# The table builder's powers go from the shared constants tile to the scratch tile of the attention

## The chip, the cores and the metric

The kernel runs on one core of a Trainium2 chip. TensorE (PE) multiplies matrices, VectorE (DVE) and ScalarE (ACT) work elementwise, GpSimd (POOL) does elementwise work too, and SyncE (SP) only starts transfers; POOL and ACT have transfer queues of their own. Each engine works through its instructions in order, and waits for another engine by a semaphore, a counter that the other engine raises. The metric is the device time of one launch in microseconds (us), as a median over runs: 3279.76 us for the kernel before, from three runs between 3275.04 and 3284.11. A difference under about 0.3% (10 us) can't be told from none.

## The reference

One sequence of 1024 tokens with 1024 channels goes through two transformer layers and then a third block, all in float32. Layer 0 mixes with forgetting attention and multi-scale pooling, layer 1 with a gated linear recurrence, and each is followed by a gated feed-forward network (FFN). The third block has an mLSTM branch and an S5 branch, a complex linear recurrence whose coefficients are computed from the inputs:

```
x = x + rmsnorm(mixer(rmsnorm(x, mix_pre_g)), mix_post_g)               # layers 0 and 1
x = x + rmsnorm((silu(h @ w_gate) * (h @ w_up)) @ w_down, ffn_post_g)   # h = rmsnorm(x, ffn_pre_g)
dt   = exp(log_dt);  mag = exp(lam_re * dt)                             # S5: parameters alone, no x
a_re = mag * cos(lam_im * dt);  a_im = mag * sin(lam_im * dt)
s_t  = a * s_(t-1) + B u_t;  y_t = Re(C s_t) + D u_t                    # complex, per group and state
```

The coefficients of S5 depend on the parameters alone, so their tables can be built at any time before the third block.

## The kernel before, in words

The channels lie on the 128 partitions and the tokens on the free axis. The 1024 tokens are two halves of 512, and a 128 x 512 tile of float32 is the unit of nearly all work. A matrix product is made of three passes: each operand is split into a rounded part and its remainder (ACT writes the first, DVE the second), and TensorE multiplies high by high, high by low and low by high. In the down projection of the FFN these are lines 632, 633 and 634; weights come in as `raw`, are split into `wsp` at lines 186 and 188, and the hidden activations `hid` are split at lines 246 and 250.

The program is written in Python generators. A main line emits the matmuls, and background generators (`start`, `tick`, `drain`) emit a few instructions of other work between them. A scheduler then sets the order on each engine and hands out memory. Tiles of one tag share a fixed number of slots: the 18 slots of `t2` (128 x 512 float32 each) hold the transfers of the hidden activations (`xt`, read by `fetch` at line 260), the temporaries `sq` and the two tiles `s5c`. A new tile in a slot must wait until every instruction that touched the tile before it there is done, whichever engine that was.

FFN 0 ends with its down projection (`ffn_down`), for token half 0 and then for half 1. The products for half 1 need 22 `hid` tiles, and each comes from a transfer `xt<-hidd` that SP issues (`hid_steps`). Beside the projection of half 0 runs the table builder, `s5_tables`:

- It takes two `s5c` tiles from `t2` (line 1239) as a pool of 64 small vectors of 16 columns; `sm(name)` hands them out in turn. POOL clears both tiles (line 1241).
- DVE computes small vectors in them, among them the eight powers `E` (real and imaginary parts, 16 vectors), each the square of the one before (lines 1281 to 1297).
- POOL builds the rotation tables `s5R` from `E` by doubling, in eight passes of two groups each. A pass clears the first column (lines 1319 and 1320), multiplies in eight steps of six instructions (lines 1326 to 1331; 1326, 1327, 1329 and 1330 read `E`), and stores two tables to DRAM by its own queue (line 1335).
- At the end SP stores the two `s5c` tiles to DRAM (line 1338); `s5_tables2` loads them later.

The tag `junk` has one slot of 1024 bytes per partition. The attention of layer 0 writes its masked scores there at line 986, where only the maximum that goes with them is used; nothing else has it before the change.

Of the kernel before, what the change touches and what calls it, by code (L numbers as in the profile page):

```python
# [11 lines left out]
F32 = mybir.dt.float32  # L12
# [55 lines left out]
class Model:  # L68
# [1166 lines left out]
    def s5_tables(self):  # L1235
# [8 lines left out]
        def sm(n):  # L1244
            i = self.s5n[n] = len(self.s5n)
            return big[i // 32][:, i % 32]
# [31 lines left out]
        V.tensor_tensor(t0, mag, mag, ALU.mult)  # L1278
        V.tensor_tensor(self.rho4, t0, t0, ALU.mult)

        E = [(sm(f"er{k}"), sm(f"ei{k}")) for k in range(8)]
        cur = (cs, sn)
        for k in range(-2, 8):
            o = E[max(k, 0)]
            if k > -2:
# [32 lines left out]
        for g0 in range(0, 16, 2):  # L1318
            G.memset(R[:, :, 0, 0:1], 1.0)
            G.memset(R[:, :, 1, 0:1], 0.0)  # L1320
            for k in range(8):
                n = 1 << k
                er, ei = (E[k][i][:, g0:g0 + 2].unsqueeze(2).to_broadcast([128, 2, n]) for i in range(2))
                s, d = slice(0, n), slice(n, 2 * n)
# [713 lines left out]
```

## Time and profile before

| | us |
|---|---|
| median of 3 runs | 3279.76 |
| the profiled execution: its own time / its span | 3275.86 / 3274.2 |
| PE busy in the span | 3099.3 (95%) |
| DVE / ACT / POOL busy | 2345.7 / 1532.8 / 803.9 |
| mean granted TensorE clock, as a share of 2.4 GHz | 0.978 |

The profile cuts the span into 40 slices of 81.9 us and gives the busy tenths of each engine. The waits say who was idle, and whose end ended the idle time; the wait of a transfer queue is told apart from the engine's own. The time line lists single instructions with their start, and the idle time ahead of them in brackets. Nearly all of the idle time of PE lies in two neighbouring slices, between 982 and 1146 us, and they are the place where the down projection of FFN 0 goes from half 0 to half 1.

### The profile page before, as it was taken

How to read it: one execution, taken by the hardware profiler on the slowest of the kernel's cores; microseconds unless marked ns; L12 is line 12 of the kernel's file. 1: busy time of each engine (PE TensorE's matmuls, PEld its weight loads, DVE VectorE, ACT ScalarE, POOL GpSimd, SP SyncE). 2: the span in 40 equal slices, each digit the busy share in tenths (PEclk: the TensorE clock that was granted, in tenths of full speed). 3: DMA queues.
4: the chain of work that ended last, by engine and by line, in shares of the span. 5: the costliest groups of instructions: out<-in, count | busy, mean ns of one | idle time of the engine just before them, and what ended most of it. 6: DMA issues, size and time to landing. Idle time of an engine off the chain costs nothing. (4 is left out here: it accounts for less than half of the span.)

```text
span 3274.2 us, 42443 instructions
## 1 busy us (share of the span) xinstructions
PE 3099.3 (95%) x14200; PEld 2526.0 (77%) x14200; DVE 2345.7 (72%) x4489; ACT 1532.8 (47%) x2842; POOL 803.9 (25%) x1002
## 2 busy tenths in 40 slices
PE   8999999999994598999999999999999999999998
PEld 5777787888883487877888887777888778778886
DVE  8768857688862359777857888786688888765664
ACT  4646644333432237676443335544455444434442
POOL 4011102555367302111236540000111100153000
PEclk9999999999997799999999999999999999999999
DMA  4443445333532434334723345576644344745562
GB/s 156 157 143 127 145 153 191 103 126 126 191 115 103 151 121 150 101 125 162 253 93 130 126 144 191 199 226 240 214 136 154 129 153 136 257 140 196 187 209 97
DMA packets 227179, 511.84 MB, mean 156 GB/s; under 512 B 28040, under 2 KB 50760, under 8 KB 226960
## 3 DMA queue, kind: packets, MB, share of 16 engines
q1 hardware_dynamic: 225680, 504.93, 46.2%
q0 software_dynamic: 1280, 4.20, 0.3%
q8 instruction: 112, 1.84, 0.2%
q14 instruction: 107, 0.88, 0.1%
HBM read 386.21 MB, written 118.59 MB: 154 GB/s over the span
## 5 line engine op out<-in xcount | busy, mean ns | idle before, releaser
L188 DVE TENSOR_TENSOR wsp<-raw,wsp 128x512 fp32r<-128x512 f32 x850 | 629.8, 747 | 350.5 <-ACT wsp L186 347.2
L186 ACT ACTIVATE wsp<-raw 128x512 fp32r<-128x512 f32 x842 | 515.7, 616 | 722.5 <-PE pd L634 201.5
L632 PE MATMUL pd<-hid,wsp 128*128 128x512 f32 x704 | 279.2, 398 | 76.6 <-ACT hid L246 76.6
L633 PE MATMUL pd<-hid,wsp 128*128 128x512 f32 x704 | 278.9, 397 | 3.5 <-DVE hid L250 3.2
L634 PE MATMUL pd<-hid,wsp 128*128 128x512 f32 x704 | 277.6, 394 | 0.0
L632 PEld LDWEIGHTS pd<-hid,wsp 128*128 128x128 f32 x704 | 133.9, 190 | 105.6 <-ACT hid L246 78.7
L495 PE MATMUL qy<-st,wsp 128*128 128x512 f32 x464 | 180.7, 389 | 3.9 <-DVE st L248 3.9
L494 PE MATMUL qy<-st,wsp 128*128 128x512 f32 x464 | 181.1, 390 | 0.2 <-ACT st L246 0.2
L496 PE MATMUL qy<-st,wsp 128*128 128x512 f32 x464 | 180.6, 389 | 0.0
L526 POOL TENSOR_TENSOR qv<-qv,qu 128x512 f32<-128x512 f32 x54 | 90.6, 1677 | 341.8 <-ACT wsp L186 226.6
L633 PEld LDWEIGHTS pd<-hid,wsp 128*128 128x128 f32 x704 | 133.9, 190 | 37.3 <-DVE hid L250 10.1
L248 POOL TENSOR_TENSOR xs<-xt,xs 128x512 fp32r<-128x512 f32 x28 | 40.8, 1457 | 483.6 <-ACT xs L246 424.8
L634 PEld LDWEIGHTS pd<-hid,wsp 128*128 128x128 f32 x704 | 134.0, 190 | 26.9
L186 ACT ACTIVATE wsp<-wss 128x512 fp32r<-128x512 f32 x108 | 68.1, 631 | 183.9 <-PE qz L496 90.3
L494 PE MATMUL pf<-xs,wsp 128*128 128x512 f32 x288 | 114.0, 396 | 9.5 <-ACT m L572 8.5
L270 DVE TENSOR_TENSOR sq<-sq 128x512 f32<-128x512 f32 x140 | 99.0, 709 | 32.1 <-ACT sq L268 31.6
L250 DVE SCALAR_TENSOR_TENSOR hid<-xt,hid 128x512 fp32r<-128x512 f32 x88 | 58.0, 689 | 84.3 <-ACT hid L246 83.6
L495 PE MATMUL pf<-xs,wsp 128*128 128x512 f32 x288 | 113.3, 394 | 0.4 <-POOL xs L248 0.4
L496 PE MATMUL pf<-xs,wsp 128*128 128x512 f32 x288 | 113.3, 394 | 0.0
L405 POOL TENSOR_TENSOR xt<-xt,m 128x512 f32<-128x512 f32 x12 | 18.2, 1524 | 364.9 <-DVE m L402 356.7
L495 PEld LDWEIGHTS qy<-st,wsp 128*128 128x128 f32 x464 | 87.1, 188 | 22.1 <-DVE st L248 4.2
L494 PEld LDWEIGHTS qy<-st,wsp 128*128 128x128 f32 x464 | 87.1, 188 | 20.3 <-DVE qu L515 1.8
(720 smaller groups left out, 9106.3 us busy)
## 6 DMA issues: line engine op xcount, KB each, us to landing
raw<-in_w_in_dram SPq DMA_DIRECT2D x86, 512.0 KB
xt<-xres SPq DMA_DIRECT2D x128, 256.0 KB
raw<-in_wd_dram SPq DMA_DIRECT2D x64, 512.0 KB
raw<-in_wg_dram SPq DMA_DIRECT2D x62, 512.0 KB
raw<-in_wu_dram SPq DMA_DIRECT2D x62, 512.0 KB
hidd<-th SPq DMA_DIRECT2D x88, 256.0 KB
xt<-hidd SPq DMA_DIRECT2D x88, 256.0 KB
raw<-in_ev_in_dram SPq DMA_DIRECT2D x32, 512.0 KB
```

Of the source, the lines that this page charges most:

```text
L186: nc.scalar.activation(sp[:, 0], raw, AF.Copy)
L188: nc.vector.tensor_tensor(sp[:, 1], raw, f(sp[:, 0]), ALU.subtract)
L248: (low or nc.vector).tensor_tensor(t[:, 1], src, f(t[:, 0]), ALU.subtract)
L250: nc.vector.scalar_tensor_tensor(t[:, 1], src, scale, f(t[:, 0]), ALU.mult, ALU.subtract)
L270: nc.vector.tensor_tensor(q, q, acc, ALU.add)
L494: nc.tensor.matmul(ps, h, xs[k][:, 0], start=start and k == 0, stop=False, skip_group_check=not start)
L495: nc.tensor.matmul(ps, h, xs[k][:, 1], start=False, stop=False, skip_group_check=not start)
L496: nc.tensor.matmul(ps, l, xs[k][:, 0], start=False, stop=k == n - 1, skip_group_check=not start)
L526: nc.gpsimd.tensor_tensor(v5, v5, u3, ALU.add)
L632: nc.tensor.matmul(ps, h_, x[:, 0], start=k0 + k == 0, stop=False)
L633: nc.tensor.matmul(ps, h_, x[:, 1], start=False, stop=False)
L634: nc.tensor.matmul(ps, l_, x[:, 0], start=False, stop=k0 + k == FFT - 1)
```

## The change

The eight powers no longer come from the `s5c` tiles. They lie in one tile of their own, `s5e`, of 16 vectors of 16 float32, which is 1024 bytes per partition; it has the tag `junk` and so the slot of the attention's scratch.

```diff
         V.tensor_tensor(t0, mag, mag, ALU.mult)
         V.tensor_tensor(self.rho4, t0, t0, ALU.mult)
 
-        E = [(sm(f"er{k}"), sm(f"ei{k}")) for k in range(8)]
+
+        et = self._t([128, 16, 16], F32, "junk", 1, "s5e")
+        E = [(et[:, 2 * k], et[:, 2 * k + 1]) for k in range(8)]
         cur = (cs, sn)
         for k in range(-2, 8):
             o = E[max(k, 0)]
```

Lines behind it move down by two. With 16 names fewer, `sm` hands out 17 vectors in all, so that the second `s5c` tile holds none; it is still cleared and stored. The instructions are the same in number, kind and shape on all engines, and the order on PE, DVE, ACT and POOL is the same, but for names. What differs is on whom some of them wait, and the place of one transfer on SP.

The first place is SP's queue, at the transfers of half 1 of the hidden activations (`hidd_15` is the 16th of 22; names such as DMAHW4 stand for transfer semaphores):

```order
 L260 DMA xt<-hidd_13_201 128x512 [waits DMAHW2_49]
 L260 DMA xt<-hidd_14_202 128x512 [waits DMAHW3_49]
-L260 DMA xt<-hidd_15_203 128x512 [waits DMAHW4_49,Pool_49]
+L260 DMA xt<-hidd_15_203 128x512 [waits DMAHW4_49]
 L260 DMA xt<-hidd_16_204 128x512 [waits DMAHW5_49,DVE_49]
 L260 DMA xt<-hidd_17_205 128x512 [waits DMAHW6_49,PE_49]
```

Nothing moved; the 16th transfer no longer waits for POOL, because POOL no longer reads the tile whose slot it takes.

The second place is DVE, in the residual addition behind the down projection of half 0 (line 405):

```order
 L188 TENSOR_TENSOR wsp<-raw,wsp 128x256 [waits Activation_49]
 L405 TENSOR_TENSOR xt<-xt,m 128x512 [waits DMAHW0_49,DVE_49]
-L405 TENSOR_TENSOR xt<-xt,m 128x512 [waits DMAHW1_49,DVE_49]
+L405 TENSOR_TENSOR xt<-xt,m 128x512 [waits DMAHW1_49,DVE_49,Pool_49]
 L402 SCALAR_TENSOR_TENSOR m<-m,pvt,rb 128x512 x2
 L188 TENSOR_TENSOR wsp<-raw,wsp 128x512 [waits DMAHW3_49,Activation_49]
```

One addition now waits for POOL too; before, DVE had waited for the same count at line 1304, where it wrote into the second `s5c` tile after POOL's clearing.

The third place is SP's queue earlier, in the middle of the down projection of half 0, where the two `s5c` tiles are stored (`s5c_675` is the second one's place in DRAM):

```order
 L175 DMA raw<-in_wd_dram 128x768 [waits DMAHW5_49,DVE_49]
-L175 DMA raw<-in_wd_dram 128x1024 [waits DMAHW6_49,DMAHW3_49,DVE_49]
-L1338 DMA s5c_675<-s5c 128x512 [waits DMAHW7_49,DVE_49]
+L1340 DMA s5c_675<-s5c 128x512 [waits DMAHW6_49,Pool_49]
+L175 DMA raw<-in_wd_dram 128x1024 [waits DMAHW7_49,DMAHW3_49,DVE_49]
 L175 DMA raw<-in_wd_dram 128x1024 [waits DMAHW4_49,DMAHW0_49,DVE_49]
```

The store of the second tile has moved ahead of one load of weights.

## Rows read from the trace of the kernel before

**Rows 1.** The page's 40 slices of the span: PE's busy tenths and granted clock.
```profile
PE   8999999999994598999999999999999999999998
PEclk9999999999997799999999999999999999999999
```

**Rows 2.** Windows: start:end, length, busy of PE, PEld, DVE, ACT, POOL; clock, DMA.
```profile
1100.00:1150.00 50.00, 49.92 (x207) 40.26 (x208) 31.35 (x50) 21.35 (x39) 0.00 (x0) 0.94 0.68 229
1150.00:1200.00 50.00, 50.00 (x227) 41.28 (x227) 22.83 (x44) 17.99 (x31) 1.81 (x2) 1.00 0.42 138
```

**Rows 3.** Waits, 950 to 1200 us: who waited for whom, total us, times, longest.
```profile
ACT hid L246 <- DMA xt<-hidd: 75.5, 4, 73.1
...
PE pd L632 <- ACT hid L246: 72.2, 1, 72.2
```

**Rows 4.** Waits of SP's transfer queue, 950 to 1200 us.
```profile
SPq L260 <- POOL s5rt L1330: 86.3, 1, 86.3
```

**Rows 5.** Time line of POOL at the tables' end: start, us, instruction, idle before.
```profile
1096.13 0.61 POOL L1330 TENSOR_TENSOR s5rt<-s5R,s5c 128x256 f32<-128x256 f32 x1
...
1097.84 1.13 POOL L1335 DMA_DIRECT2D s5r<-s5R  x2 [0.30 <-POOL s5R L1331]
1171.44 1.29 POOL L248 TENSOR_TENSOR xs<-xt,xs 128x512 fp32r<-128x512 f32 x1 [72.47 <-ACT xs L246]
```

**Rows 6.** Time line of SP's transfer queue at the join of the halves.
```profile
1096.77 3.62 SPq L260 DMA_DIRECT2D xt<-hidd  x7
```

**Rows 7.** Time line of PE around its long wait.
```profile
1027.52 0.40 PE L634 MATMUL pd<-hid,wsp 128*128 128x512 f32 x1
1100.08 0.80 PE L632 MATMUL pd<-hid,wsp 128*128 128x512 f32 x1 [72.17 <-ACT hid L246]
...
1101.40 0.63 PE L634 MATMUL pd<-hid,wsp 128*128 128x512 f32 x1
1101.83 0.63 PE L632 MATMUL pd<-hid,wsp 128*128 128x512 f32 x1
...
1106.50 0.40 PE L632 MATMUL pd<-hid,wsp 128*128 128x512 f32 x1
1106.73 0.39 PE L633 MATMUL pd<-hid,wsp 128*128 128x512 f32 x1
```

**Rows 8.** Waits of PE, 1990 to 2241 us: the same projection of FFN 1.
```profile
PE pd L632 <- ACT hid L246: 4.2, 1, 4.2
...
PE pd L633 <- DVE hid L250: 0.4, 1, 0.4
```

**Rows 9.** Windows over the multiplications of five of POOL's eight passes.
```profile
940.88:960.65 19.77, 19.77 (x89) 16.38 (x88) 6.47 (x10) 6.43 (x12) 17.00 (x50) 1.00 0.34 107
965.97:985.91 19.94, 19.94 (x90) 16.51 (x89) 6.26 (x10) 5.63 (x10) 17.17 (x50) 1.00 0.33 99
991.23:1010.82 19.59, 15.77 (x68) 12.51 (x66) 7.33 (x14) 8.24 (x14) 16.82 (x50) 0.92 0.60 205
1016.35:1036.00 19.65, 11.56 (x45) 8.16 (x43) 7.64 (x12) 6.59 (x12) 17.25 (x49) 0.85 0.00 1
1061.02:1077.77 16.75, 0.00 (x0) 0.00 (x0) 0.00 (x0) 0.00 (x0) 13.97 (x50) 0.50 0.00 0
```

**Rows 10.** Time line of POOL, start of passes 5 and 7, and the last clearing of s5c.
```profile
884.11 0.53 POOL L1241 MEMSET s5c<- 128x512 f32 x1 [0.75 <-DVE th L603]
...
1016.35 0.10 POOL L1319 MEMSET s5R<- 128x2 f32 x1 [4.39 <-DMA s5r<-s5R]
...
1061.02 0.10 POOL L1319 MEMSET s5R<- 128x2 f32 x1 [2.17 <-DMA s5r<-s5R]
```

**Rows 11.** Time line of PE at the first product of layer 1.
```profile
1212.86 0.39 PE L236 MATMUL pxr<-xs,wsp 128*128 128x512 f32 x1
```

**Rows 12.** Line groups of DVE by shape, 966 to 1011 us, then 1140 to 1170 us.
```profile
L188 DVE TENSOR_TENSOR wsp<-raw,wsp 128x512 fp32r<-128x512 f32 x14 | 10.3, 737 | 24.6 <-ACT wsp L186 24.6
...
L188 DVE TENSOR_TENSOR wsp<-raw,wsp 128x512 fp32r<-128x512 f32 x10 | 6.9, 692 | 10.4 <-ACT wsp L186 10.4
```

## The prediction, made blind

> **What bounds the kernel now.** I read the page's slices first. PE is busy in nine tenths or more of nearly every slice and at its full granted clock, so that TensorE sets the time, but for two neighbouring slices that show 4 and 5 tenths and a clock of 0.7 [rows 1]. Any change away from them touches engines that run under PE. So the question is what ends last in that hole, and the waits answer it from engine to engine: PE at line 632 waits 72.2 us for ACT's split of a hidden tile, ACT has waited 73.1 us for the transfer that brings that tile [rows 3], and the queue that starts the transfer has itself stood 86.3 us, once, for POOL at line 1330 [rows 4]. The time line closes the chain: POOL's last multiplication by a power ends at 1096.13 + 0.61 = 1096.74 us [rows 5], and SP starts the seven missing transfers at 1096.77 [rows 6]. The transfer did not want anything that POOL makes. It wanted the memory of a tile that POOL was still reading. All of POOL's passes from the fifth on are paid by everyone else.
>
> **The change, part by part.**
>
> *The wait that goes.* POOL's multiplications no longer read the `s5c` tile, so that its slot comes free when DVE has written it and SP has stored it. SP came to the 16th transfer at 1096.77 - 86.3 = 1010.5 us, and nothing behind it in that queue could start. In the changed program it goes on there. PE's idle time of 72.2 us between 1027.9 and 1100.08 [rows 7] goes with it, if the seven tiles are there in time. They are 7 x 256 KB = 1.8 MB, and around 1000 us the transfers moved 205 GB/s [rows 9], which makes 9 us: landed by about 1020 to 1023, and a split of one tile takes about 0.7 us (line 188 in [rows 12] has the same shape). PE wants the first at 1027.9. Some of the seven still wait for DVE and PE, whose work is close behind. What such a join costs where POOL is not in the way is seen in FFN 1: 4.2 and 0.4 us [rows 8]; its larger part stands at the start of the half, which here lies before the long wait and does not change. Bounds for what is left of the join: 0 to 4.6 us. I take 0.5, nearer the smaller row, since 15 of 22 tiles are already there.
>
> *The clock.* During the hole the granted clock is 0.50, TensorE's level of 1.2 GHz [rows 9], and after it matmuls start 0.43 us apart (1101.40, 1101.83) until they start 0.23 apart (1106.50, 1106.73) [rows 7]. Of the 6.42 us from 1100.08 to 1106.50 the same 15 matmuls would have taken 15 x 0.23 = 3.4, so 3.0 us come back too.
>
> *Waits that are new.* The 4th addition at line 405 waits for POOL in the changed order. The count it asks for is the one that line 1304 asked for before, POOL's second clearing, and that was over at 884.11 + 0.53 us [rows 10], over 140 us before half 1 goes on. Price 0. The store of the second `s5c` tile goes one place forward in SP's queue and waits for that same clearing: 0 as well. The slot `junk` was last used in layer 0's attention, which is done before FFN 0 begins, so taking it costs no wait. Instructions, shapes and orders are otherwise the same.
>
> *What is late next.* The tables do not get shorter; they lose a quiet machine. Before, POOL's last passes ran while DVE was idle; now half 1 of the projection runs beside them. POOL's next duty behind the tables is the low part of the input of layer 1 (line 248), which PE needs at its first product of layer 1, at 1212.86 before [rows 11], so about 1212.86 - 74.7 = 1138.2 after. Is POOL done by then? With DVE idle the multiplications of a pass take 16.75 us. Four passes beside DVE took 19.77, 19.94, 19.59 and 19.65, with DVE busy 6.47, 6.26, 7.33 and 7.64 us [rows 9]. That is 0.47, 0.51, 0.39 and 0.38 us of delay for each us of DVE, 0.44 in the mean. What DVE did in the 100 us from 1100 (31.35 + 22.83 = 54.2 us; [rows 2]) it will do from 1028 on. POOL ended at 1097.84 + 1.13 = 1099.0 [rows 5]; 54.2 x 0.44 = 23.8 us are added, and three more waits for the store between passes that are 4.39 instead of 2.17 us [rows 10], 6.7 us together. End: 1129.5. The first low part (1.29 us, [rows 5]) is there at 1130.8, 7.4 us before PE asks. So this costs 0 at the rate of the rows. The rate at which it begins to cost is (1138.2 - 1.3 - 1099.0 - 6.7) us over DVE's 54.2 and some 4 us more that it has until 1138, about 0.54, just over the largest of the four. If every us of DVE held POOL for a whole one, POOL would end 1099.0 + 6.7 + 54.2 + some 4.6 (DVE's share up to 1138) = 1164.5, and PE would stand until 1165.8: 27.6 us. Those are the bounds, 0 and 27.6; I take 0, since four rows give the rate, and keep the other end for the range.
>
> The Trainium skill has a rule against this change just here. Its page "SBUF — State Buffer", section "Who interferes with whom", says that a VectorE instruction with two SBUF inputs and a GpSimd instruction that reads SBUF shut each other out for their whole length. DVE's splits and POOL's multiplications are such a pair. The trace agrees in direction, and less in size, with 0.44 us of delay for each us; by the rule at full strength the cost would be the upper bound, 27.6 us, and by the rows it is nothing.
>
> *The other direction.* DVE's splits at line 188 took 737 ns beside POOL and 692 without it [rows 12], 0.045 us more; for the 94 DVE instructions of the 100 us [rows 2] that would be 4 us at most. DVE stood idle 10.4 us beside ten such splits, waiting for ACT [rows 12], so this stays under cover; without that cover it would cost the 4 us.
>
> **The sum.** 72.2 + 3.0 - 0.5 = 74.7 us. The profiled execution took 3275.86 us, so it would take 3201.2. The median of the runs shown is 3.9 us higher, which gives 3205.1 by that; I take the middle, 3203.
>
> **The rivals.**
>
> *POOL is late* (the case above with a rate over 0.54). For it: the margin is 7.4 us, and DVE is denser in the new neighbourhood (31.35 of 50 us) than in any of the four passes from which the rate comes. Against: the cost begins softly, at a rate of 0.6 POOL is only some 4 us late. The page of the Trainium skill named above leads to its far end. Then PE waits at line 236 for POOL at line 248, up to 27.6 us: 3205 to 3229 against the execution's own time, 3233 against the median.
>
> *Another wait takes the place.* If the addition at line 405 asked for the end of the tables, DVE would stand in half 1 from a point before 1078 (the addition lies in the first 50 us behind the hole) until at least 1099 us, and with it the weight splits and PE: 21 to 71 us, so 3222 to 3272. For it: the wait is new. Against: the count belongs to the clearing at 884 us.
>
> *The change does not do what it says.* Were the 16th transfer held by POOL through some other tile, the time would stay at 3276 to 3280. For it: POOL also holds two tiles through all its passes (`s5R`, `s5rt`). Against: these lie in slots of their own, outside `t2`, and the wait is gone from the row of the order.
>
> *Slower than before.* DVE and POOL shut each other out in both directions through half 1. If each of the 94 DVE instructions in those 100 us were held by a whole long multiplication of POOL (0.61 us, [rows 5]) with no idle time to absorb it, PE would lose 94 x 0.61 = 57 us for weights, and with POOL late by 27.6 us the loss is 85: 3201 + 85 = 3286, slower than the execution by 0.3%. It decides from 74.7 us on. Against it: splits beside POOL were longer by 0.045 us, not by 0.6, and PE was busy without a gap from 940.88 to 960.65 and from 965.97 to 985.91 beside two of POOL's passes [rows 9].
>
> **How the numbers follow.** The forecast gets 0.80, POOL late 0.13, another wait 0.03, no effect 0.03, slower 0.01. About 0.3%, or 10 us, is what a measurement of this kernel can tell from no change. Forecast, POOL late and most of the third are faster by more than that, 0.95 together; no effect and the end of the third are the same, 0.04; slower 0.01. The forecast's own range is 3197 to 3211, from the spread of the three runs (4.7 and 4.4 us on either side of their median) and the bounds of the join. Towards long times the range takes in POOL late to its end, 3233; towards short ones it reaches to 3195, which is the lowest run less 75.2 us and the spread of one run.
>
> **What would show it.** Right: SP's queue no longer waits for POOL at line 1330, and the 22 transfers go out in one stretch near 1002 to 1016 us; PE has no idle time over 5 us between 1005 and 1138; the granted clock has no 0.50 stretch there; line 236 begins near 1138. POOL's last store of a table lies near 1130, with the split of line 248 straight behind it instead of 72 us later, and PE's wait for it is not in the list. Wrong: a wait of PE at line 236 for POOL would be the first rival, and its size gives the rate; a long wait of DVE at line 405 the second; a transfer queue that stands for POOL the third; DVE splits near 1.3 us with PE waiting for `wsp` the last.

## The result, and the profile after

The changed kernel took 3201.77 us (median of 4 runs, 3198.39 to 3206.01), the kernel before 3279.6 us (4 runs, 3275.04 to 3284.11): a ratio of 0.9763, 95% interval 0.9745 to 0.9782, or 2.4% faster. The forecast was 3203, with a range of 3195 to 3233. The profiled execution took 3199.89 us with a span of 3198.2; the span forecast was 3274.2 - 74.7 = 3199.5.

The page of the changed kernel, its 40 slices of 80 us, against [rows 1]:

```profile
PE   8999999999999999999999999999999999999998
PEclk9999999999999999999999999999999999999999
```

The hole is gone, and so is the stretch at low clock behind it. PE is idle for 103.0 us of the span, where it was 174.9. The two slices of before, as one window (columns as in [rows 2]), held 77.6 us of that:

```profile
982.26:1145.97 163.71, 86.14 (x350) 68.17 (x349) 53.10 (x90) 39.68 (x70) 87.16 (x267) 0.74 0.37 127
```

That is the largest piece in one place, but not nearly all of PE's idle time, as the section on the time before has it: some 97 us lie scattered over the rest of the span, and the change does not touch them.

The next three views are of the join of the two halves: the waits of SP's queue (the longest), against [rows 4]; SP's time line, against [rows 6]; and all waits of PE from 1005 to 1142 us, against [rows 3].

```profile
SPq L175 <- DVE wsp L188: 166.6, 41, 6.9
SPq L398 <- DVE xt L405: 26.0, 16, 4.3
SPq L175 <- DVE nt L309: 5.4, 1, 5.4
```

```profile
1002.26 13.20 SPq L260 DMA_DIRECT2D xt<-hidd  x22
1015.76 14.87 SPq L175 DMA_DIRECT2D raw<-in_wd_dram  x3
```

```profile
PE sst L281 <- DVE sq L270: 2.9, 1, 2.9
PE pd L633 <- DVE hid L250: 2.8, 1, 2.8
PE rb L317 <- DVE nr L310: 0.2, 1, 0.2
```

No wait of the queue names POOL. All 22 transfers go out in 13.2 us instead of being cut after the 15th. Two of PE's waits that are left stand at the start of half 1, as before; the wait at line 632 has no remainder at all.

The time line of POOL, against [rows 5] and [rows 10] (lines behind the change are two higher: 1321 is the start of a pass, 1337 the store of its tables):

```profile
1018.95 0.10 POOL L1321 MEMSET s5R<- 128x2 f32 x1 [5.84 <-DMA s5r<-s5R]
1047.31 1.16 POOL L1337 DMA_DIRECT2D s5r<-s5R  x2 [0.30 <-POOL s5R L1333]
1052.19 0.10 POOL L1321 MEMSET s5R<- 128x2 f32 x1 [3.73 <-DMA s5r<-s5R]
...
1083.46 0.10 POOL L1321 MEMSET s5R<- 128x2 f32 x1 [4.63 <-DMA s5r<-s5R]
...
1108.96 0.10 POOL L1321 MEMSET s5R<- 128x2 f32 x1 [4.31 <-DMA s5r<-s5R]
1130.46 1.14 POOL L1337 DMA_DIRECT2D s5r<-s5R  x2 [0.30 <-POOL s5R L1333]
1131.62 5.03 POOL L248 TENSOR_TENSOR xs<-xt,xs 128x512 fp32r<-128x512 f32 x4
```

And PE's first product of layer 1, against [rows 11]:

```profile
1138.21 0.39 PE L236 MATMUL pxr<-xs,wsp 128*128 128x512 f32 x1
```

The tables end 32.6 us later than before, at 1131.6, and the splits of layer 1's input follow with no gap. PE comes to line 236 at 1138.21, 74.65 us earlier than before, and does not wait. The span is 76.0 us shorter; the 1.3 us over that lie behind 1138 and are less than the runs of one kernel differ.

What POOL and DVE cost each other is in the windows over the multiplications of passes 5 to 8, and over the 100 us from 1028, against [rows 9] and [rows 2] (length, then busy of PE, PEld, DVE, ACT, POOL):

```profile
1018.95:1047.01 28.06, 28.06 (x123) 21.96 (x123) 23.64 (x36) 16.53 (x31) 25.58 (x50) 1.00 0.59 197
1052.19:1077.38 25.19, 25.19 (x113) 20.86 (x112) 12.42 (x20) 8.94 (x17) 22.72 (x50) 1.00 0.51 165
1083.46:1103.19 19.73, 19.53 (x93) 16.08 (x92) 12.17 (x27) 6.26 (x11) 17.25 (x50) 1.00 0.45 147
1108.96:1130.16 21.20, 21.20 (x95) 17.56 (x94) 10.39 (x14) 10.48 (x19) 18.72 (x50) 1.00 0.33 101
1028.00:1128.00 100.00, 99.80 (x447) 82.25 (x447) 60.00 (x97) 40.97 (x74) 77.49 (x186) 1.00 0.54 176
```

These four windows end with the last multiplication; the one of 16.75 us with DVE idle ends 0.30 us later, where the store is issued. With 0.30 us added to each, the four passes are longer than it by 11.61, 8.74, 3.28 and 4.75 us, beside 23.64, 12.42, 12.17 and 10.39 us of DVE. PE is busy through all of it but for 0.2 us.

### The profile page after: what moved, and what is told of

Read it like the earlier page. It is cut to its first block, busy times and chain, and to the rows that moved or that the text cites. A ratio compares the mean times of both kernels' runs of the same rounds, so it can differ in the third digit from the quotient of the medians.

```text
span 3198.2 us, 42439 instructions
## 1 busy us (share of the span) xinstructions
PE 3095.2 (97%) x14200; PEld 2524.0 (79%) x14200; DVE 2348.4 (73%) x4489; ACT 1532.7 (48%) x2842; POOL 830.8 (26%) x1002
## 5 line engine op out<-in xcount | busy, mean ns | idle before, releaser
L495 PEld LDWEIGHTS qy<-st,wsp 128*128 128x128 f32 x464 | 87.2, 188 | 22.1 <-DVE st L248 4.2
L494 PEld LDWEIGHTS qy<-st,wsp 128*128 128x128 f32 x464 | 87.1, 188 | 20.7 <-DVE qu L515 1.5
L496 PEld LDWEIGHTS qy<-st,wsp 128*128 128x128 f32 x464 | 87.2, 188 | 18.1
```

The costliest lines, as they stand in the source:

```text
L494: nc.tensor.matmul(ps, h, xs[k][:, 0], start=start and k == 0, stop=False, skip_group_check=not start)
L495: nc.tensor.matmul(ps, h, xs[k][:, 1], start=False, stop=False, skip_group_check=not start)
L496: nc.tensor.matmul(ps, l, xs[k][:, 0], start=False, stop=k == n - 1, skip_group_check=not start)
```

## The experiments

Theory A is the prediction's: SP's queue stood because the 16th transfer takes a slot of `t2` that POOL read until its last multiplication, and POOL's remaining work lies under PE once nothing waits for that slot.

**Is it the slot?** First, the powers in a tile of their own, but in `t2`:

```diff
-        et = self._t([128, 16, 16], F32, "junk", 1, "s5e")
+        et = self.t2("s5e", [128, 16, 16])
```

> The changed kernel, but the tile of the powers takes one of the 18 t2 slots instead of the attention's scratch slot. Theory A (a slot of t2 is held until POOL's last multiplication, and SP's queue stands for it): the long wait is back, SP's queue stands some 86 us for POOL, PE some 72 us at line 632, time 3275 to 3283. Rival B (what helped was taking the powers out of the tile that DVE writes and SP stores): no wait comes back, time 3199 to 3206.

Measured: 3279.41 us, ratio to the kernel before 0.9999 (0.9989 to 1.0008). The longest wait of SP's queue, then the wait of PE, in the same order of views as above:

```profile
SPq L260 <- POOL s5rt L1332: 86.5, 1, 86.5
```

```profile
PE pd L632 <- ACT hid L246: 73.2, 1, 73.2
```

The wait is back in full size. That the powers have left the tile that DVE writes and SP stores is worth nothing, and rival B falls. Then the same tile in a new slot, outside both `t2` and the attention's scratch:

```diff
-        et = self._t([128, 16, 16], F32, "junk", 1, "s5e")
+        et = self._t([128, 16, 16], F32, "s5own", 1, "s5e")
```

> The changed kernel, but the tile of the powers has a new slot of 1024 bytes of its own instead of the attention's scratch slot. Theory A: any place outside t2 does the same, time 3198 to 3206, ratio to the changed kernel within 0.3%. Rival C (the scratch slot itself matters, by its place in memory or by what was there before): POOL's passes or PE's waits differ, and the time by over 10 us.

Measured: 3202.9 us, 0.9767 (0.9753 to 0.9782) of the kernel before, with POOL's tables done at 1129.4 and PE at line 236 at 1137.78. Nothing about the scratch slot itself matters to the time, and rival C falls; it was a kilobyte that nobody else needed then.

**Is it POOL's end that the slot waits for?** In the kernel before, one pass more, and then the work of four passes less:

```diff
-        for g0 in range(0, 16, 2):
+        for g0 in (0, 2, 4, 6, 8, 10, 12, 14, 14):
```

> The kernel before with POOL's eighth table pass done twice. Theory A: the whole pass, with DVE idle, is paid by SP's queue and PE: the wait at line 632 grows from 72.2 to 92 us (20.06 us a pass), time 3297 to 3303. If the transfer waited for something else, the wait and the time would stay, 3276 to 3284.

Measured: 3300.28 us, 1.0072 (1.0057 to 1.0087). The waits of SP's queue and of PE:

```profile
SPq L260 <- POOL s5rt L1330: 106.8, 1, 106.8
```

```profile
PE pd L632 <- ACT hid L246: 93.5, 2, 92.7
```

PE's longest wait grew from 72.2 to 92.7 us, by 20.5. The time grew by 23.3 us over the kernel before as it ran beside this one (3276.97 us), with an interval of 18.7 to 28.5: PE pays for the whole pass, as near as the runs can tell. The next run takes the work of four passes away:

```diff
-            for k in range(8):
+            for k in range(8 if g0 < 8 else 0):     # and no clearing from g0 = 8 on
```

> The kernel before, in which POOL's last four table passes only store what the fourth left (the tables of the second eight groups are not computed). Theory A: POOL's last read of the constants tile then ends near 985 us, before SP comes to the 16th transfer at 1010, so the wait is gone without any change of tiles: 3198 to 3206, as the changed kernel. If something else held the transfer, 3250 and more.

Measured: 3200.87 us, 0.9768 (0.9751 to 0.9784). PE's waits at the join are those of the changed kernel. The expectation was a pass too early with its 985 us: that is where the third pass ends [rows 9], and the fourth ended at 1011.5. So the queue did stand for POOL, for 1.7 us, which PE does not see:

```profile
SPq L260 <- POOL s5rt L1331: 1.7, 1, 1.7
```

```profile
PE sst L281 <- DVE sq L270: 3.0, 1, 3.0
PE pd L633 <- DVE hid L250: 2.2, 1, 2.2
```

So the whole gain of the change can be had without any change of tiles, by letting POOL be done about when SP comes to the slot. (The price there is half of the tables, which is why this is no version to keep.)

**Does POOL's work beside half 1 cost PE anything?** The same four passes taken from the changed kernel:

> The changed kernel, in which POOL's last four table passes only store what the fourth left (the tables of the second eight groups are not computed). Theory A with the prediction's terms: POOL's multiplications beside half 1 lie wholly under PE, so taking them away gives 0 to 2 us: 3198 to 3205, with DVE's splits back near 692 ns. Rival D (the two engines' meeting costs PE time in half 1): a gain of 5 to 30 us, 3170 to 3197.

Measured: 3202.35 us, 0.9763 (0.9746 to 0.9779), the same as with them. PE comes to line 236 at 1139.40, no earlier than the 1138.21 of the changed kernel. DVE's splits from 1030 to 1130 us, by shape (count, busy, mean ns), first of the changed kernel, then of this one:

```profile
L188 DVE TENSOR_TENSOR wsp<-raw,wsp 128x512 fp32r<-128x512 f32 x33 | 25.4, 771 | 26.5 <-ACT wsp L186 26.5
```

```profile
L188 DVE TENSOR_TENSOR wsp<-raw,wsp 128x512 fp32r<-128x512 f32 x33 | 23.7, 724 | 27.1 <-ACT wsp L186 27.1
```

They fell to 724 ns, not to the 692 expected; from 1030 to 1095 us, where POOL does nothing in this run, they are at 691, and what lifts the mean is one split of 1.78 us at 1129.51, beside POOL's own splits at line 248. So over the 100 us in which the tables are built, POOL lengthens a split by 0.08 us in the mean, but unevenly: in the changed kernel the mean is 818 ns from 1030 to 1045 us, 693 from 1045 to 1095 and 872 from 1095 to 1130. DVE stood idle for 26.5 us ahead of these 33 splits, waiting for ACT, and no time of PE is lost. Rival D falls.

**Is the margin at layer 1 real?** One pass more, now in the changed kernel (the loop edit above):

> The changed kernel with POOL's eighth table pass done twice. POOL then ends one pass later, about 1131.6 + 27 = 1158.6 us, and the first low part of layer 1's input is there at 1160, where PE asks for it at 1138.2. Theory (POOL late costs PE what goes over the margin of 6.6 us): PE waits 16 to 22 us at line 236 or 237 for POOL at line 248, no other wait comes, time 3216 to 3226. Rival (POOL's end has some 20 us and more of cover, since only low parts wait): under 5 us, 3199 to 3208.

Measured: 3219.53 us, 0.9823 (0.9809 to 0.9838). POOL's last store and its splits, then PE:

```profile
1153.71 1.15 POOL L1337 DMA_DIRECT2D s5r<-s5R  x2 [0.30 <-POOL s5R L1333]
1154.88 4.96 POOL L248 TENSOR_TENSOR xs<-xt,xs 128x512 fp32r<-128x512 f32 x4
```

```profile
1138.52 0.39 PE L236 MATMUL pxr<-xs,wsp 128*128 128x512 f32 x1
1156.21 0.79 PE L237 MATMUL pxr<-xs,wsp 128*128 128x512 f32 x1 [17.30 <-POOL xs L248]
```

POOL ended at 1154.9, 23 us later instead of 27; DVE did only 1.4 us of work in the 17.3 us in which PE waits. PE does the first product, which needs the high part alone, and then waits 17.3 us for the low part at line 237. The median is 17.8 us over that of the changed kernel; by the two ratios, each to the kernel before as it ran beside, it is 19.7. This is the prediction's first rival, made to happen: the wait is the one that it named, a product later (line 237, not 236), and of the 23 us some 6, the margin, cost nothing.

**Is there more in the rest of the edit?** With the powers gone the second constants tile holds nothing:

```diff
-        big = [self.t2("s5c", [128, 32, 16]) for _ in range(2)]
+        big = [self.t2("s5c", [128, 32, 16]) for _ in range(1)]   # in both table builders
```

> The changed kernel with one constants tile instead of two: the second one, which holds nothing any more, is neither cleared nor stored nor loaded. Theory A: nothing waits for it, 0 to 2 us, 3197 to 3205. A rival that t2 slots are short beside the tables would give 5 us or more.

Measured: 3204.4 us, 0.9773 (0.9758 to 0.9787), which can't be told from the changed kernel. No version that does all the work was faster than the changed kernel.

## Why the prediction was right, point by point

*The wait that goes.* Forecast 72.2 us and a remainder of 0.5 at the join; measured 72.2 and 0.0. The chain of waits, from PE to ACT to the transfer to POOL, was read rightly as one of memory and not of data, and the runs with the powers in `t2`, with a pass more and with four passes less show it from three sides.

*The clock.* Forecast 3.0 us. PE came to line 236 74.65 us earlier, although half 1 began 0.76 us later than before (its second product at 1013.15 us instead of 1012.39), so the hole and its clock gave back 75.4 us: 72.2 and 3.2. One sentence was too wide: the stretch at low clock from 1013 to 1018 us, ahead of the join, is still there, as it was before. Its granted clock is still 0.50. Only the one behind the hole went.

*Waits that are new.* Line 405's wait for POOL cost nothing: in the waits from 950 to 1200 us no DVE instruction stands for POOL.

*What is late next.* The forecast was 1129.5 us for the end of the tables; it was 1131.6. The call was right, but its parts were less good than their sum. One of the four rows behind the rate was read short: its window stops at 1036.00 us, and pass 5 multiplied on for another 1.3 us before it stored its tables. First the store, then the whole window of the pass, up to the store like the others of [rows 9]:

```profile
1037.58 1.15 POOL L1335 DMA_DIRECT2D s5r<-s5R  x2 [0.30 <-POOL s5R L1331]
```

```profile
1016.35:1037.58 21.23, 11.56 (x45) 8.16 (x43) 7.64 (x12) 6.59 (x12) 18.45 (x50) 0.82 0.00 1
```

That pass was 4.48 us longer than 16.75, not 2.90, a rate of 0.59 and not 0.38. So the break-even of 0.54 does not lie just over the largest of the four, as the prediction argued; it lies under it, and that POOL is done in time rests on the mean alone. The four rows then give 0.49 in the mean, an end at about 1132 us and a margin of under 5 us. Measured were 28.4 us of delay on 58.6 us of DVE, a rate of 0.48, with 0.49, 0.70, 0.27 and 0.46 in the single passes, one of them over the break-even. The margin, forecast 7.4 us, was 1138.21 - 1131.62 - 1.3 = 5.3.

The end lies 32.6 us later than before, and three terms make it up. The four passes are together 23.9 us longer than before, where 23.8 had been forecast; that this agrees is in part luck, since the rate was too low and the 54.2 us of DVE were too many (within the passes DVE's busy time rose by 51.0 us, from the 7.6 of pass 5 to 58.6). The stores between the passes took 6.1 us more, forecast 6.7, with waits of 4.2 us each. And pass 5 began 2.6 us later than before, which had no term: 1.15 us were there when pass 4 stored its tables, and the rest is a longer wait for that store, 5.84 us instead of 4.39. From 1005 to 1018.4 us the transfers that no longer stand in the queue keep the DMA engines busier (a share of 1.02 instead of 0.80); in the three runs whose queue stands for POOL, the kernel before among them, this wait was 4.39 to 4.80 us, and 5.84 to 6.45 in the four with all passes whose queue does not.

*The other direction.* Forecast were 0.045 us more for a split of DVE, and 4 us at most in all. A split was 0.08 us longer in the mean; all of DVE's work in the 100 us came to 60.0 us, against 56.45 with four passes less, so the price in all was 3.55 us. It stayed under cover, as forecast: the run with four passes less is no faster.

*The rule that spoke against the change.* The Trainium skill, "SBUF — State Buffer", section "SBUF: two separate sides", says that the one of the two engines that comes second is blocked for the whole instruction. The trace agrees in one place, and for longer than one instruction (the last section); over a pass it came to 0.48 us for each us of DVE, and the full price of 27.6 us at line 236 did not come. Why the rate is below one was not tried.

*The sum.* 74.7 forecast against 76.0 in span. The median fell by 77.8, with an interval of 71.5 to 83.6.

## What to carry to other kernels

When a transfer queue stands for an engine that makes nothing the transfer needs, look at who last read the slot that it fills: a small operand inside a rotating buffer holds the whole slot until its slowest reader is done, and on an in-order queue it holds all that is behind it. Move the long-lived operand to memory that nothing else wants in that time; of the two places that were tried, one did as well as the other. Then look at the engine whose work loses its quiet stretch, and compute when its next consumer asks. Where a rate is read from windows, see that each window ends where the work in it ends.

## What the runs showed of the hardware that was not expected

A multiplication of 128 x 2 elements on POOL, which takes 0.19 us, took 4.55 us in the changed kernel. POOL's time line, then DVE's beside it:

```profile
1052.37 4.55 POOL L1328 TENSOR_TENSOR s5rt<-s5R,s5e 128x2 f32<-128x2 f32 x1
1056.88 0.19 POOL L1329 TENSOR_TENSOR s5rt<-s5R,s5e 128x2 f32<-128x2 f32 x1
```

```profile
1051.98 0.68 DVE L270 TENSOR_TENSOR sq<-sq 128x512 f32<-128x512 f32 x1
1052.58 0.68 DVE L188 TENSOR_TENSOR wsp<-raw,wsp 128x512 fp32r<-128x512 f32 x1
1053.18 0.68 DVE L270 TENSOR_TENSOR sq<-sq 128x512 f32<-128x512 f32 x1
1053.79 0.68 DVE L405 TENSOR_TENSOR xt<-xt,m 128x512 f32<-128x512 f32 x1
1054.39 0.68 DVE L188 TENSOR_TENSOR wsp<-raw,wsp 128x512 fp32r<-128x512 f32 x1
1054.99 1.28 DVE L405 TENSOR_TENSOR xt<-xt,m 128x512 f32<-128x512 f32 x2
1056.19 0.68 DVE L188 TENSOR_TENSOR wsp<-raw,wsp 128x512 fp32r<-128x512 f32 x1
```

DVE has eight instructions of two SBUF inputs back to back, each started before the one ahead has ended, and POOL's ends with the last of them. So the block here is not one instruction long but as long as the chain; DVE's own instructions were no longer than 0.68 us. The same instruction took 3.85 us in the run with a slot of its own and 4.49 us in the one with one constants tile, beside the same chain. But in the run with the extra pass the same eight instructions stood there back to back, from 1052.04 to 1056.95 us, and POOL, which began in their midst, got through between them:

```profile
1053.25 0.73 POOL L1328 TENSOR_TENSOR s5rt<-s5R,s5e 128x2 f32<-128x2 f32 x1
1053.93 0.67 POOL L1329 TENSOR_TENSOR s5rt<-s5R,s5e 128x2 f32<-128x2 f32 x1
1054.68 0.53 POOL L1330 TENSOR_TENSOR s5R<-s5rt 128x2 f32<-128x2 f32 x1
1055.28 0.52 POOL L1331 TENSOR_TENSOR s5rt<-s5R,s5e 128x2 f32<-128x2 f32 x1
```

Each took 0.52 to 0.73 us there, and DVE's no more than 0.69. So such a chain can hold POOL to its end, as in three traces, and need not, as in the fourth. What decides between the two is open.
